# A hybrid trunk layer: input products made of un-normalised h, with the norm's factor applied where each block leaves PSUM

## The chip, the core and the metric

The kernel runs on one core of one Trainium2 chip. A core has TensorE (PE in the profile; PEld is its weight load), VectorE (DVE), ScalarE (ACT), GpSimd (POOL) and SyncE (SP, which here only issues the transfers), each with its own instruction queue that runs in order. The metric is the device time of one execution in microseconds.

## The reference, cut to what matters

One layer over T = 528 tokens (16 learned ones and 512 of the sequence), 1024 channels wide:

```python
u = rmsnorm(h, norm_mix[l])               # h * rsqrt(mean(h*h) + eps) * gain
proj = u @ w_in[l]
feat_rw, feat_fx, gate_part = ...         # recurrent group, attention group, gates
gates = sigmoid(gate_part + b_gate[l])
y_rw = rwkv7_branch(feat_rw, ...)         # begins f + mu * (token_shift(f) - f)
y_fx = fox_branch(feat_fx, ...)           # q and k get a head rmsnorm
merged = gates[..., :D] * (y_rw @ w_out_rw[l]) + gates[..., D:] * (y_fx @ w_out_fx[l])
h = h + merged @ w_o[l]
h = h + square(relu(rmsnorm(h, norm_mlp[l]) @ w_up[l])) @ w_down[l]
```

The factor of rmsnorm is one number per token. A product with u is therefore the product with gain * h, times that number for each token. Channels lie on partitions and tokens along the columns, so the factor is a row of T numbers, the same on all partitions.

## The kernel before, in words

**Precision.** Every large product takes both operands as a high and a low part (`whi`, `wlo`, `uhi`, `ulo`) and three passes: high by high, high by low, low by high. The high part is a copy on ACT, the low part a subtraction on DVE or GpSimd.

**Blocks.** The input projection is cut into 42 blocks of 128 output channels: two lora blocks (`B_LORA`, `B_GD`), then for each of four pairs of heads three attention blocks (query, key, value) and three recurrent ones (key, receptance, value: tiles `okk`, `orr`, `ov`), then 16 gate blocks. A block is 8 k-slices x 3 passes per part of the tokens. A part is 264 columns (HT), so two parts make a block; gates and queries take one part of 512. PSUM has two banks for them (`ppj`, tag "pj").

**Opening (L304 to L402).** For each half of the tokens: squares on ACT (L332), sums of them on DVE (L339, L342), h times the gain split into `uhi` and `ulo` (L335, L336), the forget products `pf` (L347), the sum over channels by a product with ones (L350), and the factor `rs` as Ln and Exp on ACT (L352, L353). The first two blocks are made of this un-normalised h and multiplied by `rs` in PSUM (L361). Then h is normalised in place, and split once more (L371 to L374), for all other blocks. The first two blocks pass Tanh (L399, L400), are split into `lhi` and `llo`, and feed the lora products of `decay` (L680).

```python
V.scalar_tensor_tensor(xt[t][:, k, :], xt[t][:, k, :], pr[:, ...], rss[t], ALU.mult, ALU.mult)   # L371
A.copy(uhi[:, kk, tk], xt[t][:, kk, :])                                                          # L373
V.tensor_tensor(ulo[:, kk, tk], xt[t][:, kk, :], uhi[:, kk, tk].bitcast(F32), ALU.subtract)      # L374
```

**Token shift (L297 to L300).** A recurrent block leaves PSUM in two steps: ACT writes mu * block into a tile `tm`, one column to the right (L298), and DVE adds (1 - mu) * block to it (L299).

**Middle.** Several streams of work run beside one another: `recurrent` (decay, keys, rows, scores, the inverse of a triangular matrix, bonus), `chain` (the recurrence over nine chunks), `group_norm`, `fox_features`, `attention`, and `projections`, which makes the asked blocks by rank: recurrent first, attention next, gates last (L446 to L475). `Turns` writes PE's order from them: a model clock (`Clock`) guesses when each step's inputs are ready, and the stream of the best rank that can go on is written next. The order on PE is then fixed (`manual_schedule`), while the other engines' instructions are placed by the scheduler, with more priority for streams of rank 0 and 1. Gates are stored to DRAM with their bias added (L481, L482).

**Merge (L1021 to L1038).** For each of 8 blocks m and both branches (br), a gate is loaded (`gl`, two buffers for each branch), passes Tanh, and is multiplied with the branch's product `po` (four PSUM buffers); GpSimd adds the branches and the sum is split.

```python
nc.sync.dma_start(g, gates_d[8 * br + m])                                   # L1026
act(g, g, AF.Tanh, scale=0.5)                                               # L1027
...                                                                         # 12 products into po, L1032
V.scalar_tensor_tensor(g, g, 1.0, po, ALU.add, ALU.mult)                    # L1034
...
G.tensor_tensor(pp[0], pp[0], pp[1], ALU.add)                               # L1036
merged = act(mhi[:, m, :], pp[0], AF.Copy, scale=0.5)                       # L1037
V.scalar_tensor_tensor(mlo[:, m, :], pp[0], 0.5, mhi[...], ALU.mult, ALU.subtract)   # L1038
```

The product with w_o (L1064) follows, whose four results take the four `po` buffers, then its second half (L1081) and the MLP (L1115, L1148).

Of the kernel before, what the change touches and what calls it, by code (L numbers as in the profile page):

```python
# [182 lines left out]
def kernel(ctx, tc, ht, x, win, par, cst, gain, lora, wout, wo, wup, wdn, out, dbg=None):  # L183
# [20 lines left out]
    pr1 = cp.tile([128, 14], F32, name="pr1")  # L204
    prh = cp.tile([128, 4, 4], F32, name="prh")
# [57 lines left out]
    with ExitStack() as st:  # L263
# [13 lines left out]
        def proj(blk, evac, parts=((0, HT), (HT, T)), w=None):  # L277

            w = w or load_w(win[blk], (G, V))
            for a0, a1 in parts:  # L280
                po = ppj("pj")[:, :a1 - a0]
                n = 0
                for k in range(KB):
                    for a, b in passes(wk(w, k), U):
                        mm(po, a, b[:, k, a0:a1], start=n == 0, stop=n == 23)
                        n += 1
                evac(po, slice(a0, a1))

# [3 lines left out]
        def tshift(blk, dst):  # L292

            tm = rp.tile([128, 1 + T], F32, name="tm")
            V.memset(tm[:, 0:1], 0.0)

            def evac(po, sl):  # L297
                act(tm[:, sl.start + 1:sl.stop + 1], po, AF.Copy, scale=pr[:, C_MU + blk:C_MU + blk + 1])  # L298
                V.scalar_tensor_tensor(dst[:, sl], po, pr1[:, blk:blk + 1], tm[:, sl], ALU.mult, ALU.add)  # L299
            return evac  # L300

# [10 lines left out]
        lfs = [rp.tile([128, TP], F32, name=f"lf{i}", tag=("okk", "orr")[i]) for i in range(2)]  # L312
        with tc.tile_pool(name="xp", bufs=2) as xp:
# [3 lines left out]
            nc.sync.dma_start(pr, par)  # L317
            for c in range(4):
                nc.sync.dma_start(xt[0][:, 2 * c:2 * c + 2, :].rearrange("p a b -> p (a b)"), ht[0, c])
            w_lora = load_w(win[B_LORA], (G, G))  # L320
            for c in range(4):
                nc.sync.dma_start(xt[1][:, 2 * c:2 * c + 2, :].rearrange("p a b -> p (a b)"), ht[1, c])
            w_gd = load_w(win[B_GD], (G, G))
# [3 lines left out]
            rss = []  # L327
            for t in range(2):
                tk = slice(HT * t, HT * t + HT)
                for c in range(4):  # L330
                    sq = xp.tile([128, 2, HT], F32, name="sq", bufs=3)
                    act(sq, xt[t][:, 2 * c:2 * c + 2, :], AF.Square)  # L332
                    for k in range(2 * c, 2 * c + 2):
                        gn = pr[:, C_GN + k:C_GN + k + 1]
                        act(uhi[:, k, tk], xt[t][:, k, :], AF.Copy, scale=gn)  # L335
                        V.scalar_tensor_tensor(ulo[:, k, tk], xt[t][:, k, :], gn, uhi[:, k, tk].bitcast(F32), ALU.mult, ALU.subtract)  # L336
                    if c == 0:
                        acc = xp.tile([128, HT], F32, name="acc")
                        V.tensor_tensor(acc, sq[:, 0, :], sq[:, 1, :], ALU.add)  # L339
                    else:  # L340
                        for k in range(2):
                            V.tensor_tensor(acc, acc, sq[:, k, :], ALU.add)  # L342
                pf = psm("pf")[:8, :HT]
                n = 0
                for k in range(KB):
                    for a, b in passes([x[:, 8 * k:8 * k + 8] for x in wf], U):
                        mm(pf, a, b[:, k, tk], start=n == 0, stop=n == 23)  # L347
                        n += 1
                pq = psm("pss")[:, :HT]
                mm(pq, ones, acc, start=True, stop=True)  # L350
                rs = xp.tile([128, HT], F32, name="rs")
                act(rs, pq, AF.Ln, bias=eps, scale=1.0 / 1024)  # L352
                act(rs, rs, AF.Exp, scale=-0.5)  # L353
                rss.append(rs)
                V.tensor_tensor(f0[:, tk], pf, rs[:8], ALU.mult)
                if t == 0:
                    V.tensor_scalar(pr1, pr[:, C_MU:C_MU + 14], -1.0, 1.0, ALU.mult, ALU.add)
                    shift = tshift(12 + B_LORA, lfs[0])

                def normed_shift(po, sl):  # L360
                    V.tensor_tensor(po, po, rss[sl.start // HT], ALU.mult)  # L361
                    shift(po, sl)

                proj(B_LORA, normed_shift, ((tk.start, tk.stop),), w_lora)
            shift = tshift(12 + B_GD, lfs[1])
            proj(B_GD, normed_shift, w=w_gd)
            for t in range(2):
                tk = slice(HT * t, HT * t + HT)
                for c in range(4):
                    for k in range(2 * c, 2 * c + 2):  # L370
                        V.scalar_tensor_tensor(xt[t][:, k, :], xt[t][:, k, :], pr[:, C_GN + k:C_GN + k + 1], rss[t], ALU.mult, ALU.mult)  # L371
                    kk = slice(2 * c, 2 * c + 2)
# [858 lines left out]
```

## Time and profile before

| | |
|---|---|
| median of 3 runs | 937.02 us (935.64 to 938.87) |
| the profiled execution's own time | 937.56 us |
| its span in the trace | 935.6 us |
| mean granted PE clock | 0.967 |
| PE busy | 882.0 us, 94% |
| first block product of the middle | at 42.76 us |
| first product of the merge | at 486.76 us |
| first product of the MLP (L1115) | at 581.24 us |

Times are microseconds from the start of the span. A row of a timeline gives start, length, engine, line and operation, then output and inputs by the program's names, and in brackets how long the engine idled before and what it waited for. A row of groups gives the count after x, the busy time, and the mean in ns. Matmuls are pipelined: the distance from one start to the next counts, not a row's length. "Clock" is the share of full speed that PE was granted.

### The profile page before, as it was taken

Reading aid. Unit: us, or ns where it says so; the run is one execution under the profiler, and the core shown is the slowest. Engines: PE = TensorE matmul, PEld = TensorE weight load, DVE = VectorE, ACT = ScalarE, POOL = GpSimd, SP = SyncE. Lnnn points to the kernel's source line nnn. Section 1 sums busy time; section 2 is a strip of 40 time slices with the busy share of each in tenths; the row PEclk is TensorE's granted clock in tenths of the full one; section 3 lists DMA queues with packets and bytes.
Section 4 is the critical chain, followed back from the end, with each engine's and each line's share of the span. In section 5 each row is a group of like instructions: output and inputs, shape, how many; then the busy total and the mean of one; then the engine's idle time right before and its main releaser. Section 6 shows DMA issues by size and latency. Waiting matters only on the chain.

```text
span 935.6 us, 15452 instructions
## 1 busy us (share of the span) xinstructions
PE 882.0 (94%) x5964; PEld 721.1 (77%) x5964; DVE 515.2 (55%) x1052; ACT 422.3 (45%) x885; POOL 158.3 (17%) x145
## 2 busy tenths in 40 slices
PE   6589889999888999999979999999999999999998
PEld 4578777688777778678758778988888888888886
DVE  7974875548869861663356755354423244443322
ACT  7746342677354535746454553344322233442221
POOL 4253333213232332113302200000000000000000
PEclk9789899899889999999989999999999999999999
DMA  5121112111011132112247650122232222222331
GB/s 204 46 69 47 46 49 86 58 58 45 28 46 35 61 117 81 47 58 90 80 154 262 212 174 9 43 94 101 90 102 93 99 101 92 101 98 94 119 118 57
DMA packets 45449, 83.30 MB, mean 89 GB/s; under 512 B 5048, under 2 KB 6200, under 8 KB 45376
## 3 DMA queue, kind: packets, MB, share of 16 engines
q1 hardware_dynamic: 45376, 82.32, 25.8%
q8 instruction: 47, 0.77, 0.3%
q14 instruction: 26, 0.21, 0.1%
HBM read 75.99 MB, written 6.31 MB: 88 GB/s over the span
## 4 chain that ended last, share of the span: by engine, by line
PE 79%; DVE 12%; ACT 3%; DMA 3%; issue 2%; POOLq 0%; SPq 0%; DVEq 0%; ACTq 0%
PE pj L470 21%; PE po L1115 19%; PE pd L1148 19%; PE po L1032 4%; PE po L1081 2%; PE pw L822 2%; PE psc L574 1%; PE py L619 1%; DVE xt L371 1%; DVE L L726 1%; DVE L L724 1%; PE ppt L605 1%; PE pbt L770 1%; PE pch L887 1%; PE psr L755 1%
## 5 line engine op out<-in xcount | busy, mean ns | idle before, releaser
L231 DVE TENSOR_TENSOR wlo<-wraw,whi 128x512 fp32r<-128x512 f32 x148 | 104.9, 710 | 177.1 <-ACT whi L230 175.2
L230 ACT CAST whi<-wraw 128x512 fp32r<-128x512 f32 x152 | 94.0, 620 | 192.1 <-PE pd L1148 109.6
L470 PE MATMUL pj<-uhi,whi 128*128 128x264 f32 (+1 forms) x480 | 169.5, 353 | 3.8 <-DVE orr L299 2.6
L470 PE MATMUL pj<-uhi,wlo 128*128 128x264 f32 (+1 forms) x480 | 158.7, 331 | 0.0
L470 PE MATMUL pj<-ulo,whi 128*128 128x264 f32 (+1 forms) x480 | 158.6, 330 | 0.0
L442 POOL TENSOR_TENSOR wlo<-wraw,whi 128x512 fp32r<-128x512 f32 x80 | 108.4, 1359 | 251.6 <-ACT whi L441 244.1
L470 PEld LDWEIGHTS pj<-uhi,whi 128*128 128x128 f32 x480 | 94.8, 197 | 24.1 <-issue 10.6
L470 PEld LDWEIGHTS pj<-uhi,wlo 128*128 128x128 f32 x480 | 94.6, 197 | 7.2
L1148 PE MATMUL pd<-whi,fhi 128*128 128x512 f32 x256 | 99.6, 389 | 0.0
L1148 PE MATMUL pd<-wlo,fhi 128*128 128x512 f32 x256 | 99.6, 389 | 0.0
L1148 PE MATMUL pd<-whi,flo 128*128 128x512 f32 x256 | 99.6, 389 | 0.0
L470 PEld LDWEIGHTS pj<-ulo,whi 128*128 128x128 f32 x480 | 95.2, 198 | 4.9
L1115 PE MATMUL po<-zhi,whi 128*128 128x512 f32 (+1 forms) x248 | 94.8, 382 | 0.0
L1115 PE MATMUL po<-zlo,whi 128*128 128x512 f32 (+1 forms) x248 | 94.8, 382 | 0.0
L1115 PE MATMUL po<-zhi,wlo 128*128 128x512 f32 (+1 forms) x248 | 94.8, 382 | 0.0
L441 ACT CAST whi<-wraw 128x512 fp32r<-128x512 f32 x80 | 49.5, 619 | 57.1 <-PE pj L470 36.4
L1148 PEld LDWEIGHTS pd<-wlo,fhi 128*128 128x128 f32 x256 | 48.1, 188 | 10.0
L1148 PEld LDWEIGHTS pd<-whi,fhi 128*128 128x128 f32 x256 | 48.1, 188 | 10.0
L1148 PEld LDWEIGHTS pd<-whi,flo 128*128 128x128 f32 x256 | 48.1, 188 | 9.9
L1115 PEld LDWEIGHTS po<-zlo,whi 128*128 128x128 f32 x248 | 46.6, 188 | 9.1
L1115 PEld LDWEIGHTS po<-zhi,whi 128*128 128x128 f32 x248 | 46.6, 188 | 9.0
L1115 PEld LDWEIGHTS po<-zhi,wlo 128*128 128x128 f32 x248 | 46.6, 188 | 9.0
(277 smaller groups left out, 1461.6 us busy)
## 6 DMA issues: line engine op xcount, KB each, us to landing
wraw<-in_win SPq DMA_DIRECT2D x84, 256.0 KB, 2.6
wraw<-in_wup SPq DMA_DIRECT2D x64, 256.0 KB, 2.6
wraw<-in_wdn SPq DMA_DIRECT2D x64, 256.0 KB, 2.5
gd<-gt SPq DMA_DIRECT2D x16, 256.0 KB, 2.1
wraw<-in_wout SPq DMA_DIRECT2D x16, 256.0 KB, 4.0
gl<-gd SPq DMA_DIRECT2D x16, 256.0 KB, 3.4
wraw<-in_wo SPq DMA_DIRECT2D x16, 256.0 KB, 3.3
xt<-in_ht SPq DMA_DIRECT2D x8, 264.0 KB, 4.6
```

Source lines behind the costliest of these rows:

```text
L230: A.copy(hi, raw)
L231: low.tensor_tensor(lo, raw, hi.bitcast(F32), ALU.subtract)
L371: V.scalar_tensor_tensor(xt[t][:, k, :], xt[t][:, k, :], pr[:, C_GN + k:C_GN + k + 1], rss[t], ALU.mult, ALU.mult)
L441: A.copy(hi, raw)
L442: G.tensor_tensor(lo, raw, hi.bitcast(F32), ALU.subtract)
L470: mm(po, a, b[:, k, a0:a1], start=n == 0, stop=n == 23)
L574: mm(sc, q[hs, 128 * i:128 * i + 128], k[hs, a:b], start=True, stop=True)
L822: mm(ps_[hs, n - b0, :], lhs(n)[hs], rhs(n)[hs], start=True, stop=True)
L1032: mm(po, a, b[:, k, :], start=n == 0, stop=n == 11)
L1081: mm(po, a[:, k, 128 * i:128 * i + 128], b[:, k, :], start=n == 0, stop=n == 23)
L1115: mm(po[:, t0:t1], a, b[:, k, t0:t1], start=n == 0, stop=n == 23)
L1148: mm(pd[i], a[:, b_, 128 * i:128 * i + 128], b, start=b_ == 0 and n == 0, stop=b_ == 15 and n == 2)
```

## The change

The in-place normalisation goes, and `uhi`, `ulo` stay un-normalised for all blocks. The factor `rs` is kept for all T tokens and applied

- to recurrent blocks by DVE in PSUM, ahead of the token shift; the shift now has ACT write (1 - mu) * block and DVE add mu times the column to the left, in place, without `tm`. So the second part starts two columns earlier (`SHIFTED`);
- to query, key and value blocks by DVE on the way out of PSUM (queries and keys are squared from SBUF after it);
- to gates after they are loaded back, by GpSimd; their bias moves into Tanh's bias operand (`bgh`).

In the opening the two lora blocks and the forget products are made together, k-slice by k-slice, in an order written out by hand (PE's manual order now begins there), the second half of tokens in the two banks that the recurrence uses later; weights are loaded in between h's slices, and DVE makes their low parts. Every block's evacuation gets the scheduler's priority, the model clock is read around it, the lora products wait in the model for `lhi` and `llo` (set to 5.0), and the inverse gives way to other streams at every second step.

```diff
+    bgh = cp.tile([128, 16], F32, name="bgh")
+    rs = cp.tile([128, T], F32, name="rs")
...
             def evac(po, sl):
-                act(tm[:, sl.start + 1:sl.stop + 1], po, AF.Copy, scale=pr[:, C_MU + blk:C_MU + blk + 1])
-                V.scalar_tensor_tensor(dst[:, sl], po, pr1[:, blk:blk + 1], tm[:, sl], ALU.mult, ALU.add)
+                n, x = sl.stop - sl.start, 2 if sl.start else 0
+                V.tensor_tensor(po, po, rs[:, sl], ALU.mult)
+                act(dst[:, sl.start + x:sl.stop], po[:, x:], AF.Copy, scale=pr1[:, blk:blk + 1])
+                x = x or 1
+                d = dst[:, sl.start + x:sl.stop]
+                V.scalar_tensor_tensor(d, po[:, x - 1:n - 1], pr[:, C_MU + blk:C_MU + blk + 1], d, ALU.mult, ALU.add)
             return evac
+        manual = st.enter_context(ExitStack())
+        manual.enter_context(tc.manual_schedule(engines={mybir.EngineType.PE}))
...
+            load_x(0, 0)
+            w2 = [[], []]
+            for j in range(2):
+                for i, blk in enumerate((B_LORA, B_GD)):
+                    w2[i].append(load_h(win[blk][:, 512 * j:512 * j + 512], V, "w", (4, 4, 4)))
+                load_x(0, 1 + j)
+            load_x(0, 3)
             for c in range(4):
+                load_x(1, c)
...
+                    for j in range(3):
+                        for a, b, dst, cols in [(*passes([x[:, 8 * k:8 * k + 8] for x in wf], U)[j], pf, tk)] + [(*passes(wk(w2[i], k), U)[j], pls[i], sl) for i in range(2)]:
+                            mm(dst, a, b[:, k, cols], start=n == 0, stop=n == 23)
                         n += 1
...
+                for j in range(2):
+                    mm(pq, ones, acc[:, j, :], start=j == 0, stop=j == 1)
+                act(rs[:, tk], pq, AF.Ln, bias=eps, scale=1.0 / 1024)
+                act(rs[:, tk], rs[:, tk], AF.Exp, scale=-0.5)
...
-            for t in range(2):
-                tk = slice(HT * t, HT * t + HT)
-                for c in range(4):
-                    for k in range(2 * c, 2 * c + 2):
-                        V.scalar_tensor_tensor(xt[t][:, k, :], xt[t][:, k, :], pr[:, C_GN + k:C_GN + k + 1], rss[t], ALU.mult, ALU.mult)
-                    kk = slice(2 * c, 2 * c + 2)
-                    A.copy(uhi[:, kk, tk], xt[t][:, kk, :])
-                    V.tensor_tensor(ulo[:, kk, tk], xt[t][:, kk, :], uhi[:, kk, tk].bitcast(F32), ALU.subtract)
...
+        for t_ in (lhi, llo):
+            ck.w[t_.tensor.name] = 5.0
...
+        SHIFTED = ((0, HT), (HT - 2, T))
...
-                        evac(po, slice(a0, a1))
+                        ck.read()
+                        ck.urgent = True
+                        with tc.high_priority():
+                            evac(po, slice(a0, a1))
+                        ck.read()
+                        ck.urgent = False
...
-                    act(gt, po, AF.Identity, bias=pr[:, C_BG + i:C_BG + i + 1])
+                    A.copy(gt, po)
...
-                            d["s"] = act(sq[:, sl], po, AF.Square)
-                            A.copy(f[:, sl.start - c0:sl.stop - c0], po)
+                            x = f[:, sl.start - c0:sl.stop - c0]
+                            V.tensor_tensor(x, po, rs[:, sl], ALU.mult)
+                            d["s"] = act(sq[:, sl], x, AF.Square)
...
-                    return lambda po, sl: A.copy(d["v"][:, sl], po)
+                    return lambda po, sl: V.tensor_tensor(d["v"][:, sl], po, rs[:, sl], ALU.mult)
...
-                    yield lambda: max(ck.ready(*lw), banks(2))
+                    yield lambda: max(ck.ready(*lw, lhi, llo), banks(2))
...
             for s in range(15):
+                if s % 2:
+                    yield lambda: ck.ready(AX_) - 2.0
...
                 nc.sync.dma_start(g, gates_d[8 * br + m])
-                act(g, g, AF.Tanh, scale=0.5)
+                G.tensor_tensor(g, g, rs[:, NM:], ALU.mult)
+                act(g, g, AF.Tanh, bias=bgh[:, 8 * br + m:8 * br + m + 1], scale=0.5)
```

More of the change, by code (lines that the diff above doesn't have):

```diff
@@ L275 @@
         U = (uhi, ulo)
[L277 to L286, printed above, removed]
-                evac(po, slice(a0, a1))
         SEQ = ((NM, T),)
@@ L311 @@
         f1 = rp.tile([8, T], F32, name="f1", tag="sq")
-        lfs = [rp.tile([128, TP], F32, name=f"lf{i}", tag=("okk", "orr")[i]) for i in range(2)]
+        lfs = [rp.tile([128, T], F32, name=f"lf{i}", tag=("okk", "orr")[i]) for i in range(2)]
         with tc.tile_pool(name="xp", bufs=2) as xp:
@@ L326 @@
             split(wf[0], wf[1], pr[:, C_FL:])
-            rss = []
+            V.tensor_scalar(pr1, pr[:, C_MU:C_MU + 14], -1.0, 1.0, ALU.mult, ALU.add)
+            shifts = [tshift(12 + blk, lfs[i]) for i, blk in enumerate((B_LORA, B_GD))]
             for t in range(2):
                 tk = slice(HT * t, HT * t + HT)
-                for c in range(4):
-                    sq = xp.tile([128, 2, HT], F32, name="sq", bufs=3)
-                    act(sq, xt[t][:, 2 * c:2 * c + 2, :], AF.Square)
-                    for k in range(2 * c, 2 * c + 2):
[L334 to L342, printed above, removed]
+                sl = slice(tk.start - 2 * t, tk.stop)
@@ L348 @@
                         n += 1
                 pq = psm("pss")[:, :HT]
[L350 to L358, printed above, removed]
@@ L375 @@
+                act(rs[:, tk], pq, AF.Ln, bias=eps, scale=1.0 / 1024)
+                act(rs[:, tk], rs[:, tk], AF.Exp, scale=-0.5)
+                V.tensor_tensor(f0[:, tk], pf, rs[:8, tk], ALU.mult)
+                for i in range(2):
+                    shifts[i](pls[i], sl)
         y_rw = yp.tile([128, 4, S], F32, name="y_rw")
@@ L381 @@
         V.tensor_scalar(prh[:, 3, :], pr[:, C_KA:C_KA + 4], -0.5, 1.0, ALU.mult, ALU.add)
+        V.tensor_scalar(bgh, pr[:, C_BG:C_BG + 16], 0.5, None, ALU.mult)
         V.tensor_scalar(qg8, pr[:, C_QG:C_QG + 1], 0.125, None, ALU.mult)
@@ L395 @@
         dump("F", fF)
-        lf, gf = (x[:, :T] for x in lfs)
+        lf, gf = lfs
         act(lf[:64], lf[:64], AF.Tanh)
@@ L658, in begin @@
                     return tshift(3 * self.p + i, pad(t))
-                return ask(1, self.b0 + i, begin, need=need)
+                return ask(1, self.b0 + i, begin, SHIFTED, need)
             def ask_keys(self, need=None):
@@ L995 @@
             ask(9, B_GATE + i, gate_job(i), SEQ)
-        with tc.manual_schedule(engines={mybir.EngineType.PE}):
-            turns.run()
+        turns.run()
+        manual.close()
         dump("y_rw", y_rw.rearrange("p a b -> p (a b)"))
```

31 lines of the change are left out of this document (14 added, 17 removed).

## The prediction

> **What bounds the kernel now.** I read the engine table first, then the chain that ended last, then the stretches between the stage borders, then what TensorE (PE) waits for.
>
> ```profile
> PE 882.0 (94%) x5964; PEld 721.1 (77%) x5964; DVE 515.2 (55%) x1052; ACT 422.3 (45%) x885; POOL 158.3 (17%) x145
> PE 79%; DVE 12%; ACT 3%; DMA 3%; issue 2%; POOLq 0%; SPq 0%; DVEq 0%; ACTq 0%
> ```
>
> PE is busy for 94% of the span and holds 79% of the chain, so time can be won or lost only where PE idles or runs at a low clock. The stretches say where. Columns: length, then busy time (and instructions) of PE, weight load, VectorE (DVE), ScalarE (ACT), GpSimd (POOL), then granted clock.
>
> ```profile
> 0.00:42.70 42.70, 23.43 (x160) 17.93 (x160) 36.89 (x83) 31.34 (x60) 14.43 (x21) 0.93 0.40 137
> 42.70:482.20 439.50, 414.88 (x3782) 334.97 (x3780) 277.01 (x670) 225.14 (x537) 132.13 (x116) 0.94 0.18 59
> 482.20:600.00 117.80, 112.01 (x562) 93.78 (x563) 69.52 (x105) 58.48 (x112) 11.75 (x8) 0.97 0.46 158
> 600.00:935.60 335.60, 331.70 (x1464) 274.40 (x1462) 131.75 (x196) 107.29 (x179) 0.00 (x0) 1.00 0.29 98
> ```
>
> PE idles 42.7 - 23.4 = 19.3 us in the opening, 24.6 us in the long middle, 5.8 us around the merge, and little after 600, where nothing of the change lies. The change can touch three stretches: it shortens the opening, puts multiplications into the middle, and puts a GpSimd multiplication into the merge.
>
> **The opening, -2.9 us.** Removed are the lines that normalise h in place.
>
> ```profile
> L371 DVE SCALAR_TENSOR_TENSOR xt<-xt,pr,rs 128x264 f32<-128x264 f32 x16 | 10.0, 660 | 0.0
> L374 DVE TENSOR_TENSOR ulo<-xt,uhi 128x528 fp32r<-128x528 f32 x8 | 5.5, 694 | 0.0
> ...
> L361 DVE TENSOR_TENSOR pj<-pj,rs 128x264 f32<-128x264 f32 x4 | 1.7, 428 | 0.0
> ```
>
> ```profile
> 41.37 0.59 PE L680 MATMUL pup<-llo,lw 64*128 64x264 f32 x2 [7.72 <-DVE llo L255]
> 42.76 0.59 PE L470 MATMUL pj<-uhi,whi 128*128 128x264 f32 x1
> ```
>
> That is 15.5 us of DVE work, in front of llo, for which PE waits 7.72 us; the first block product starts at 42.76. It is not 15.5 us of time, because other things are late next. First, PE: the changed opening has the same 144 products, now strictly in one order, each block's k-slices for all three targets, and four sums of squares instead of two.
>
> ```profile
> 5.77 0.39 PE L347 MATMUL pf<-uhi,wf 128*8 128x264 f32 x1 [5.77 <-ACT uhi L335]
> ...
> 25.02 0.28 PE L285 MATMUL pj<-uhi,whi 128*128 128x264 f32 x1
> ...
> 27.44 0.28 PE L285 MATMUL pj<-uhi,wlo 128*128 128x264 f32 x1
> ```
>
> ```profile
> L335 ACT ACTIVATE uhi<-xt,pr 128x264 fp32r<-128x264 f32 x16 | 7.3, 504 | 0.0
> ...
> L332 ACT ACTIVATE sq<-xt 128x528 f32<-128x528 f32 x8 | 5.1, 635 | 1.3 <-DMA xt<-in_ht 1.3
> ```
>
> From 25.02 to 27.44 are 20 steps, 0.121 us each. 144 such are 17.4 us; from the same start at 5.8, with about 2 us for the four sums and 2.5 us for the slow first products and the first weights' split (an estimate), PE ends near 27.7. ACT's 12.4 us of squares and splits and four weight casts are done near 19, so they, DVE's splits (four weight splits come over to it from GpSimd), and h's slices, which SP now loads behind the weights, all hide under PE. Then comes a serial ACT chain, in the compiled order: Ln, Exp, (DVE multiplies), the bias, two shifts, Exp, table load, Tanh, table load, Ln, table load, Tanh, the split.
>
> ```profile
> 25.10 0.48 ACT L352 ACTIVATE rs<-pss,eps 128x264 f32<-128x264 f32 x1 [0.25 <-PE pss L350]
> ...
> 29.31 1.28 ACT L399 ACT_TABLE_LOAD   x1
> 30.61 0.65 ACT L399 ACTIVATE lf<-lf 64x528 f32<-64x528 f32 x1
> ```
>
> Three loads of 1.28, some eight activations of 0.45 to 0.65 and three DVE steps of 0.4 to 0.7 make about 10.7: llo near 38.4. The twelve lora products ahead of the first block product took 42.76 - 41.37 = 1.4, so it starts at 39.85, 2.9 us sooner. The weights of the first blocks are converted by then on ACT and GpSimd. Bounds: -6 if PE warms at once and the chain overlaps, -0.5 if the cold start lasts. PE still waits some 10 us there, so the slow restart stays:
>
> ```profile
> 43.15 0.42 PE L470 MATMUL pj<-ulo,whi 128*128 128x264 f32 x1
> ...
> 46.89 0.41 PE L470 MATMUL pj<-uhi,whi 128*128 128x264 f32 x1
> ```
>
> Seventeen steps of 0.22 instead of 0.121: 1.7 us, spent now and after. The Trainium skill (TensorE: Matmul & The Clock Gate, "HAM oscillation") says that idle gaps of over about 3.4 us throttle PE, and the trace agrees: a wait of 7.72 us, then half speed. By that rule a long wait that the change adds costs some 2 us more than itself; that lies inside my bounds below.
>
> **The middle, -1.2 us.** Every block leaving PSUM is now multiplied by the factor on DVE: 24 recurrent parts and 16 key and value parts at 0.43 (L361), 4 query blocks of twice the width (by the same rate 0.8): 20 us more DVE on top of 277.0 of 439.5, while ACT loses its plain copies. A part takes 24 x 0.121 = 2.9 us on PE, there are two banks, and the evacuation (DVE, ACT, DVE instead of ACT, DVE) still fits when DVE is free; behind a long DVE instruction it doesn't. Where DVE is already the limit PE waits:
>
> ```profile
> PE psr L755 <- DVE L L726: 1.5, 1, 1.5
> PE pj L470 <- DVE orr L299: 1.3, 1, 1.3
> PE psr L755 <- DVE L L759: 0.8, 1, 0.8
> ```
>
> The compiled PE order answers partly: 138 block products instead of 126 stand ahead of the first pair's score products, 120 instead of 114 ahead of the second's: 18 x 0.121 = 2.2 us of filled wait. The value copy, for which PE waited 3.0 (below), moves to DVE with priority: I take half, 1.5. Against it I set 2.5 us for DVE's 20: it runs 63% busy over the stretch, and an eighth of the added work is what I let meet a waiting PE, the 0.26 us that two more columns in 288 products cost among it. The evacuations wait for PE at the head of DVE's queue, with the inverse's and the rows' instructions behind them. Bounds: -8 (a third of the 24.6 us idle goes), +8 (four tenths of the added work is late).
>
> ```profile
> PE pv L544 <- ACT vf L533: 3.0, 1, 3.0
> ```
>
> **Into the merge, +1.5 us.** PE's order now ends the middle with 45 gate products after the last attention product; before, the last attention followed the last gate.
>
> ```profile
> 480.88 0.69 ACT L481 ACTIVATE gt<-pj,pr 128x512 f32<-128x512 f32 x1 [0.96 <-PE pj L470]
> ...
> 486.09 0.62 ACT L230 CAST whi<-wraw 128x512 fp32r<-128x512 f32 x1 [0.22 <-DMA wraw<-in_wout]
> ```
>
> ```profile
> 486.76 0.80 PE L1032 MATMUL po<-yhi,whi 128*128 128x512 f32 x1 [4.59 <-ACT whi L230]
> ```
>
> The merge's first weights are loaded on SP's queue behind the last gate's store, in both kernels. From the last gate's evacuation to the first merge product took 486.76 - 480.88 = 5.9 us, of which PE waited 4.59 and had 1.3 of attention. Now it has none of that, and waits it all. Bounds 0 to +2.
>
> **The merge, +7.5 us.** The factor is applied to each gate by GpSimd. Two multiplications per m are 16 more of the size of its addition, and the compiled GpSimd order puts the addition of m behind the multiplication of m+1 (m from 1 to 4). That multiplication waits for a DMA into the buffer that m-1 gives back only after its addition, mhi and mlo: a ring, once per m.
>
> ```profile
> L1027 ACT ACTIVATE gl<-gl x16: 615/632/636, 488.9 to 531.7; 128x512 f32<-128x512 f32 x16
> ...
> L1036 POOL TENSOR_TENSOR gl<-gl,gl x8: 1276/1446/1799, 495.3 to 535.5; 128x512 f32<-128x512 f32 x8
> L1037 ACT ACTIVATE mhi<-gl x8: 615/628/635, 497.0 to 537.2; 128x512 fp32r<-128x512 f32 x8
> L1038 DVE SCALAR_TENSOR_TENSOR mlo<-gl,mhi x8: 684/692/693, 497.6 to 537.8; 128x512 fp32r<-128x512 f32 x8
> ...
> DMA to landing us min/median/max: 2.5/3.4/5.7
> ```
>
> ```profile
> 495.34 1.60 POOL L1036 TENSOR_TENSOR gl<-gl,gl 128x512 f32<-128x512 f32 x1 [31.18 <-DVE gl L1034]
> 500.71 1.29 POOL L1036 TENSOR_TENSOR gl<-gl,gl 128x512 f32<-128x512 f32 x1 [3.77 <-DVE gl L1034]
> ```
>
> By the medians (the middle ones of three, in ns) a turn is 0.63 + 0.69 + 3.4 + 1.45 + 1.45 and 0.1 of hops, 7.7 us. PE needs less per m:
>
> ```profile
> 532.39 0.39 PE L1064 MATMUL po<-whi,mhi 128*128 128x512 f32 x1
> ...
> 534.25 0.50 PE L1064 MATMUL po<-whi,mhi 128*128 128x512 f32 x1 [0.34 <-DVE gl L1034]
> ```
>
> 192 products from 486.76 to 532.39, 45.6 us, about 5.5 per m once warm (24 steps of 0.228). The first addition ends 10.2 us into the stage (495.34 + 1.60 - 486.76). Four turns of 7.7 give 41.0; the loads, multiplications and additions of m 5 to 7 follow at 47.4 and 53.7, the last multiplication at 55.2, Tanh and the two last products with po at 57.9. Four po buffers hide this from PE until m is 6 or so, but L1064 needs all four at its start (the 0.34 above is already that wait). Its last 87 products take 19.8 us: end at 77.7, against 68.0 now: +9.7. With a landing of 3.0 (towards the shortest) and GpSimd at its shortest, 1.28, the same sum gives +5.2; I take 7.5, between them, as DMA is less busy there without the loads of x, which come earlier now. At the shortest of all rows (2.5 and 1.28) it is +2.2, at GpSimd's longest (1.8) +14.
>
> ```profile
> L231 DVE TENSOR_TENSOR wlo<-wraw,whi 128x512 fp32r<-128x512 f32 x148 | 104.9, 710 | 177.1 <-ACT whi L230 175.2
> ```
>
> ```profile
> 500.76 1.79 DVE L231 TENSOR_TENSOR wlo<-wraw,whi 128x512 fp32r<-128x512 f32 x1
> ```
>
> The weight split beside a GpSimd addition took 1.79 us against a mean of 0.71: it waited for GpSimd, so the new multiplications also delay weights, and may be held up themselves (rival 5). The Trainium skill (SBUF — State Buffer, "Who interferes with whom") calls this an exclusive lock between GpSimd and a DVE instruction with two SBUF inputs, whole instructions long. This row agrees; by that rule, held throughout, the stage would take the long GpSimd durations, +14 instead of +7.5.
>
> **Sum.** -2.9 - 1.2 + 1.5 + 7.5 = +4.9 us on the profiled execution's own 937.56 (span 935.6 and 2.0 around it): 942.5. That execution lies 0.5 above the median of 937.02, so for the median I say 942.0.
>
> **Rivals.**
> 1. The middle pays: PE's new order and evacuations with priority remove waits and slow restarts that I left standing. For it: 24.6 us of idle, and clocks below 0.95 beside each wait. Against it: DVE, the engine waited for, gets 20 us more. It decides from about -8 in the middle with a ring at its short rows: -2.9 - 8 + 1.5 + 2.2 = -7.2, 930, faster.
> 2. The terms cancel: the ring costs 5.2 or less and the middle gives 3: -2.9 - 3 + 1.5 + 5 = +0.6, 938.
> 3. DVE becomes the bound of the middle: its heavy parts are full (9.39 of 10 us at 100 to 110), and +8 there gives 951 with the ring.
>
> ```profile
> 100.00:110.00 10.00, 6.85 (x57) 6.03 (x57) 9.39 (x14) 2.06 (x4) 4.56 (x6) 0.93 0.17 53
> ```
>
> 4. The opening gains nothing, since PE's cold start or the table loads take it all: 945, with the ring.
> 5. GpSimd and DVE hold each other up through the merge, each GpSimd instruction at its longest, 1.8: +14 there, 948.5.
>
> **Numbers.** A measurement of this kernel can tell about 0.3% (2.8 us) from no change. Forecast 942, with the ring as worked out: 0.38; rival 1: 0.27; rival 2: 0.20; rivals 3 and 4: 0.08 together; rival 5: 0.07. The forecast's lower edge reaches into no change, so: faster 0.27, the same 0.23, slower 0.50. Leaving out about a tenth on each side, rival 1's far part and that of rivals 3 and 5, the range is 929 to 951.
>
> **What would show it.** Opening: the first block product near 39.9 (right), under 37 or over 42 (wrong). Middle: its idle near 24 us, the wait for the value copy halved. Merge: GpSimd's additions 7 to 8 us apart, PE waiting for DVE's gl at the start of L1064 (L1066 in the new file) for several us; if that wait is under 2 us, the ring is wrong, and the kernel is level or faster. A first merge product less than 5 us after the last gate product would refute the third term.

## The result, and the profile after

The changed kernel takes **964.17 us** (962.75 to 965.86) against 937.46 for the kernel before on the same chips: ratio 1.028, 95% interval 1.025 to 1.031. It is 26.7 us slower. The forecast was 942.0 (929 to 951): the sign is right, the size is not.

The engine table and the chain of the changed kernel, to be held against those of before (882.0 us of PE, 94%; DVE 12% of the chain):

```profile
PE 888.8 (92%) x5968; PEld 724.1 (75%) x5968; DVE 525.4 (55%) x1055; ACT 413.3 (43%) x857; POOL 172.4 (18%) x157
...
PE 76%; DVE 14%; ACT 3%; DMA 2%; issue 2%; POOL 2%; SPq 0%; DVEq 0%; ACTq 0%; POOLq 0%
```

The span grew by 28.3 us and PE's busy time by 6.8, so most of the loss is waiting. I cut the span at three events: the first block product, the first merge product, and the first product of the second half of w_o. Between the first two lies the **middle**, between the last two the **merge**. Columns as in the prediction: length, busy time of PE, weight load, DVE, ACT, GpSimd, granted clock. Middle and merge of the kernel before:

```profile
42.80:486.80 444.00, 414.82 (x3783) 334.97 (x3781) 281.62 (x677) 229.33 (x545) 132.13 (x116) 0.94 0.18 62
486.80:556.00 69.20, 68.11 (x289) 55.07 (x289) 43.96 (x64) 37.65 (x64) 11.75 (x8) 0.97 0.66 227
```

Opening, middle, merge and rest of the changed kernel:

```profile
0.00:40.30 40.30, 23.44 (x164) 19.87 (x164) 23.27 (x56) 29.38 (x55) 8.12 (x18) 0.88 0.44 145
40.30:504.10 463.80, 417.66 (x3783) 335.08 (x3781) 302.38 (x707) 224.25 (x528) 135.64 (x119) 0.94 0.19 63
504.10:584.40 80.30, 72.27 (x288) 56.24 (x289) 47.99 (x64) 36.80 (x61) 28.64 (x20) 0.93 0.56 180
584.40:963.90 379.50, 375.46 (x1737) 312.92 (x1736) 151.79 (x229) 122.84 (x216) 0.00 (x0) 1.00 0.27 89
```

The opening gives 2.4 us, the middle costs 19.8 and the merge 11.1; the rest is level. In the middle DVE has 20.8 us more, as the prediction counted, and PE idles 46.1 us instead of 29.2. The four largest of PE's waits there (total, times, longest):

```profile
PE psr L754 <- DVE BK L713: 7.2, 2, 3.6
PE pv L543 <- DVE vf L532: 5.6, 2, 3.1
PE psr L754 <- DVE L L758: 5.5, 6, 1.2
PE ppt L602 <- DVE rsum L588: 4.9, 1, 4.9
```

All of these name DVE. In the kernel before, PE waited 3.0 us for the value copy (`vf`), and not at all for the keys (`BK`). The next rows show the fourth wait. PE, in the changed kernel, around the first inverse, and the edges of opening and merge:

```profile
37.79 0.59 PE L679 MATMUL pup<-lhi,lw 64*128 64x264 f32 x2 [10.03 <-ACT lhi L256]
...
40.33 0.59 PE L462 MATMUL pj<-uhi,whi 128*128 128x264 f32 x1
...
144.57 0.55 PE L543 MATMUL pv<-cs,vf 128*128 128x128 f32 x3 [3.09 <-DVE vf L532]
155.60 0.37 PE L602 MATMUL ppt<-cs,pe 128*16 128x128 f32 x1 [4.87 <-DVE rsum L588]
...
504.08 0.79 PE L1034 MATMUL po<-yhi,whi 128*128 128x512 f32 x1 [6.17 <-ACT whi L232]
```

DVE at the same place:

```profile
146.34 4.49 DVE L817 COPY Tt<-TT 32x576 f32<-32x576 f32 x4
150.84 2.60 DVE L817 COPY AX<-AX 32x576 f32<-32x576 f32 x4
...
153.68 0.49 DVE L582 TENSOR_TENSOR psc<-psc,cs 128x128 f32<-128x128 f32 x2
...
154.96 0.16 DVE L588 RECIPROCAL rsum<-rsum 128x1 f32<-128x1 f32 x1 [0.35 <-ACT pe L587]
```

The inverse gave way, so PE's order has the first attention step of pair 0 inside it; but on DVE that attention's scores stand behind the inverse's last copies, and PE stands still until 155.60, in front of a product that nothing can pass.

### The profile page after: what moved, and what is told of

The parts are those of the page before. It is cut to its first block, busy times and chain, and to the rows that moved or that the text cites. A ratio compares the mean times of both kernels' runs of the same rounds, so it can differ in the third digit from the quotient of the medians.

```text
span 963.9 us, 15442 instructions
## 1 busy us (share of the span) xinstructions
PE 888.8 (92%) x5968; PEld 724.1 (75%) x5968; DVE 525.4 (55%) x1055; ACT 413.3 (43%) x857; POOL 172.4 (18%) x157
## 4 chain that ended last, share of the span: by engine, by line
PE 76%; DVE 14%; ACT 3%; DMA 2%; issue 2%; POOL 2%; SPq 0%; DVEq 0%; ACTq 0%; POOLq 0%
PE pj L462 19%; PE po L1117 18%; PE pd L1150 18%; PE po L1066 2%; PE po L1083 2%; DMA gl<-gd 2%; PE pw L823 1%; DVE tmp L805 1%; DVE AX L806 1%; PE psc L573 1%; DVE L L723 1%; POOL gl L1028 1%; PE py L618 1%; POOL gl L1038 1%; DVE Bm L757 1%
## 5 line engine op out<-in xcount | busy, mean ns | idle before, releaser
L233 DVE TENSOR_TENSOR wlo<-wraw,whi 128x512 fp32r<-128x512 f32 x152 | 108.6, 715 | 182.4 <-ACT whi L232 180.8
L462 PE MATMUL pj<-uhi,whi 128*128 128x264 f32 (+2 forms) x480 | 170.4, 355 | 2.4 <-DVE orr L291 2.4
L462 PE MATMUL pj<-ulo,whi 128*128 128x264 f32 (+2 forms) x480 | 158.6, 330 | 0.0
L462 PE MATMUL pj<-uhi,wlo 128*128 128x264 f32 (+2 forms) x480 | 158.1, 329 | 0.0
L462 PEld LDWEIGHTS pj<-uhi,whi 128*128 128x128 f32 x480 | 94.3, 197 | 22.0 <-issue 10.2
```

The costliest lines, as they stand in the source:

```text
L233: low.tensor_tensor(lo, raw, hi.bitcast(F32), ALU.subtract)
```

## The experiments

Times are medians; ratios are to the kernel before on the same chip (937.5 to 938.9 us), with 95% intervals. Stages come from one profiled execution each, which in e3 and e18 was some 5 us shorter than the median, and in e10 and e16 8 and 4 us longer: they show the place, the median the price. Opening, middle and merge are as above.

| run | us | ratio (interval) | opening | middle | merge |
|---|---|---|---|---|---|
| before | 937.5 | | 42.8 | 444.0 | 69.2 |
| changed | 964.2 | 1.028 (1.025-1.031) | 40.3 | 463.8 | 80.3 |
| e1 | 965.2 | 1.029 (1.024-1.034) | 40.5 | 461.1 | 80.4 |
| e2 | 954.3 | 1.018 (1.015-1.021) | 40.6 | 453.7 | 77.9 |
| e3 | 973.6 | 1.037 (1.033-1.042) | 41.1 | 465.1 | 80.6 |
| e4 | 955.4 | 1.018 (1.013-1.022) | 41.9 | 461.7 | 69.8 |
| e5 | 952.6 | 1.016 (1.013-1.019) | 40.8 | 461.1 | 68.9 |
| e6 | 948.1 | 1.010 (1.007-1.013) | 40.9 | 458.2 | 68.3 |
| e7 | 954.4 | 1.017 (1.015-1.020) | 43.1 | 459.6 | 70.6 |
| e8 | 945.6 | 1.008 (1.006-1.010) | 40.5 | 454.9 | 68.8 |
| e9 | 938.6 | 1.001 (0.999-1.002) | 42.7 | 446.3 | 70.3 |
| e10 | 973.3 | 1.039 (1.035-1.044) | 42.8 | 487.1 | 69.8 |
| e11 | 944.8 | 1.008 (1.007-1.010) | 43.0 | 441.5 | 79.4 |
| e12 | 946.8 | 1.011 (1.009-1.013) | 41.4 | 456.0 | 67.8 |
| e13 | 945.6 | 1.008 (1.006-1.010) | 42.8 | 454.7 | 69.4 |
| e14 | 942.7 | 1.005 (1.003-1.006) | 42.7 | 449.9 | 69.0 |
| e15 | 944.8 | 1.007 (1.005-1.008) | 41.3 | 452.2 | 68.9 |
| e16 | 986.9 | 1.050 (1.048-1.052) | 41.0 | 487.6 | 80.7 |
| e17 | 948.8 | 1.012 (1.009-1.015) | 40.4 | 448.4 | 77.7 |
| e18 | 949.9 | 1.012 (1.010-1.015) | 41.7 | 444.1 | 77.3 |

### First: load, order, priority, merge

Theory A was that DVE's added work itself costs the middle; theory B that the new order does.

**e1**, a thin factor (8 of a recurrent part's columns are multiplied, the others left as they are):

```diff
-                V.tensor_tensor(po, po, rs[:, sl], ALU.mult)
+                c = n if blk >= 12 else 8
+                V.tensor_tensor(po[:, :c], po[:, :c], rs[:, sl.start:sl.start + c], ALU.mult)
```

> Recurrent blocks are multiplied by the factor in 8 of their 264 columns only (the rest of the factor is left out for them), while the planner's model is still charged for the whole width, so that PE's order stays that of the changed kernel, instruction for instruction; about 8 us of DVE's work in the middle go. Theory A (the middle's 17 us come from DVE's added work, met by a waiting PE): the middle of 456.8 us gets 5 to 10 us shorter, 954 to 959 in all. Theory B (they come from PE's new order, above all the inverse that gives way and the evacuations with priority; the work itself is hidden): at most 2 us, 962 to 964.

DVE lost 7.9 us in the middle (302.38 to 294.47), the middle 2.7, the median nothing. Theory A falls as far as the recurrent blocks' load goes.

**e2**, no giving way:

```diff
             for s in range(15):
-                if s % 2:
-                    yield lambda: ck.ready(AX_) - 2.0
```

> The inverse no longer gives way at every second step, as in the kernel before; all else as changed. Theory A: the middle stays within 3 us of 456.8, 961 to 967 in all. Theory B: 8 us or more come back, under 956.

The middle lost 10.1 us, and the wait of 4.87 is gone. The median, 954.3, is as theory B had it.

**e3**, no priority (the bare `evac(po, slice(a0, a1))` again):

> Evacuations without the scheduler's priority and without the reading of the model clock around them, as in the kernel before. Theory A: no gain, or a loss, since the longer evacuation then waits behind other DVE work: 962 to 970. Theory B: DVE's rows, keys and inverse are no longer pushed back, the middle gets 6 us or more shorter, under 958.

9 us slower by the median, 2 by its profiled execution, so the priority is no cost here. Theory B is right on the giving way alone.

**e4**, gates early:

```diff
                     A.copy(gt, po)
+                    G.tensor_tensor(gt, gt, rs[:, NM:], ALU.mult)
...
-                G.tensor_tensor(g, g, rs[:, NM:], ALU.mult)
                 act(g, g, AF.Tanh, bias=bgh[...], scale=0.5)
```

> GpSimd multiplies each gate by the factor before it is stored, in the middle, instead of after it is loaded back in the merge; PE's order is the same, instruction for instruction. If the ring on GpSimd is what makes the merge longer (80.3 us from its first product to the first of the w_o product's second half, 69.2 before), the stage comes back to 69 to 71 and the whole gains 9 to 11 less what 21 us of added GpSimd work cost the middle: 953 to 957. If the merge is longer because its weights come late or the clock is low, the stage stays above 76 and the whole above 960.

The merge is back at 69.8. The ring is all but 0.6 us of the merge's loss. GpSimd in the merge of the changed kernel, two turns of it:

```profile
532.19 1.29 POOL L1028 TENSOR_TENSOR gl<-gl,rs 128x512 f32<-128x512 f32 x1 [2.83 <-DMA gl<-gd]
534.12 1.30 POOL L1028 TENSOR_TENSOR gl<-gl,rs 128x512 f32<-128x512 f32 x1 [0.64 <-DMA gl<-gd]
535.38 1.74 POOL L1038 TENSOR_TENSOR gl<-gl,gl 128x512 f32<-128x512 f32 x1
539.94 1.29 POOL L1028 TENSOR_TENSOR gl<-gl,rs 128x512 f32<-128x512 f32 x1 [2.83 <-DMA gl<-gd]
541.93 1.28 POOL L1028 TENSOR_TENSOR gl<-gl,rs 128x512 f32<-128x512 f32 x1 [0.69 <-DMA gl<-gd]
543.17 1.73 POOL L1038 TENSOR_TENSOR gl<-gl,gl 128x512 f32<-128x512 f32 x1
```

Addition to addition takes 7.79 us. GpSimd idles 2.83 in each turn for a load that could only be issued after the last addition.

### Second: do the pieces add up?

**e5**, e2 and e4 together. **e6**, e5 without the factor. **e8**, e5 with queries and keys unscaled (evacuation as before: Square and copy on ACT).

> The two edits that helped, together: the inverse doesn't give way, and gates are multiplied by the factor before they are stored. If they are separate costs, the gains of 9.8 and 8.8 us add up: 944 to 947. If the GpSimd work that comes into the middle collides with the inverse or the weight splits there, less than 14 of the 18.6 are seen: over 950.

> As the kernel with both edits, but the factor is left out for all recurrent, query, key and value blocks; queries, keys and values leave PSUM on ACT as in the kernel before; evacuations keep their priority. Theory A (what is left of the middle's loss, 8 to 10 us, is the multiplications in the evacuation): the middle up to the merge takes at most 446 us, 935 to 939 in all. Theory D (it is the rest of the new order and the priority): it stays above 450, 942 to 947.

> As the kernel with both edits, but queries and keys leave PSUM without the factor (Square and copy on ACT, as in the kernel before): their own head norm divides it out again, up to its eps. 6.6 us of DVE's work go. Theory A: a third of the remaining loss comes back, 941 to 944. Theory D: no change against the kernel with both edits, 944 to 947.

They don't add up: e5 has the merge of e4 but a middle of 461.1, 7.4 more than e2, though GpSimd's 21 us cost nothing beside the giving way (e4). Leaving out all multiplications (18 us of DVE) brings only 2.9 back (e6; 4.5 by the medians), nearer to theory D; leaving out those of queries and keys alone brings 6.2 (e8; 7.0 by the medians). A piece's price depends on the order that it meets. So I turned round and put single parts into the kernel before.

**e7**, the giving way alone in the kernel before (the two lines of e2):

> The kernel before, with one edit of the change alone: the inverse gives way at every second step. If the giving way is a cost of its own, the middle up to the merge (444.0 us) gets 7 to 12 us longer, 945 to 950 in all. If it costs only beside longer evacuations, it stays within 3 us: 935 to 941.

15.6 us in the middle, a cost of its own, and more than either forecast. Here it falls elsewhere. PE, then the granted clock in the stretches behind it:

```profile
223.02 0.28 PE L470 MATMUL pj<-uhi,wlo 128*128 128x264 f32 x1
230.53 1.06 PE L942 MATMUL pyt<-cs,y_rw 128*64 128x128 f32 x4 [7.23 <-DVE y_rw L935]
```

```profile
217.00:223.00 6.00, 6.00 (x70) 5.18 (x69) 4.57 (x11) 5.11 (x15) 1.46 (x2) 1.00 0.01 3
...
233.00:235.50 2.50, 1.71 (x18) 1.14 (x18) 1.19 (x4) 0.53 (x2) 0.00 (x0) 0.50 0.00 0
235.50:238.00 2.50, 2.50 (x27) 1.97 (x24) 0.58 (x2) 1.07 (x5) 0.00 (x0) 0.50 0.00 0
```

PE's order now has the group norm's transposes early, while DVE is still on keys and the norm's small steps; 7.23 us of waiting, then half clock.

### Third: one part alone in the kernel before

**e9**, the new opening alone, with h normalised in place behind it:

> The kernel before with the new opening alone: lora blocks and forget products made together in the written order, weights between h's slices; h is then normalised in place as before, and PE's order of the middle is that of the kernel before, instruction for instruction. If the opening's gain of 2.4 us is its own, the first block product starts at 40 to 41 and the whole takes 934 to 936.5. If the in-place normalisation, left standing, holds llo or the first slices up, it starts after 42.3 and the whole takes 937 or more.

The gain is gone: first block product at 42.7. The rows of PE say why: `lhi` comes 1.1 us later than in the changed kernel (38.92, not 37.79), and the wait for `llo` behind it is 1.77, not 0.55, because ACT and DVE also normalise.

```profile
38.92 0.59 PE L683 MATMUL pup<-lhi,lw 64*128 64x264 f32 x2 [10.12 <-ACT lhi L254]
41.28 0.59 PE L683 MATMUL pup<-llo,lw 64*128 64x264 f32 x2 [1.77 <-DVE llo L255]
42.68 0.59 PE L473 MATMUL pj<-uhi,whi 128*128 128x264 f32 x1
```

**e10**, the multiplications alone (by one):

```diff
+                if blk < 12:
+                    V.tensor_tensor(po, po, one..., ALU.mult)
                 act(tm[:, sl.start + 1:sl.stop + 1], po, AF.Copy, scale=...)
...
-                            d["s"] = act(sq[:, sl], po, AF.Square)
-                            A.copy(f[...], po)
+                            V.tensor_tensor(x, po, one..., ALU.mult)
+                            d["s"] = act(sq[:, sl], x, AF.Square)
...
-                    return lambda po, sl: A.copy(d["v"][:, sl], po)
+                    return lambda po, sl: V.tensor_tensor(d["v"][:, sl], po, one..., ALU.mult)
```

> The kernel before with the multiplications alone: every recurrent, query, key and value block is multiplied by one on DVE where it leaves PSUM (in PSUM ahead of the token shift; on the way to SBUF for the others, in place of ACT's copy), 20 us more of DVE's work, nothing else changed. Theory A (the work on DVE costs by itself): the middle up to the merge, 444.0 us, gets 4 to 9 us longer, 941 to 947. If the cost lies in the giving way alone: at most 2 us, 936 to 940.

Neither theory: 43 us in the middle for 14 us more of DVE (36 us by the medians). What PE waited for, and the place:

```profile
PE pw L827 <- DVE AX L821: 29.0, 4, 15.7
```

```profile
130.00:140.00 10.00, 3.37 (x28) 3.15 (x26) 9.13 (x28) 4.04 (x6) 2.65 (x2) 0.82 0.16 52
140.00:150.00 10.00, 0.44 (x2) 0.29 (x2) 9.67 (x17) 0.59 (x2) 1.41 (x1) 0.50 0.05 13
```

For over 15 us PE has nothing to do but wait for the inverse (`pw` is its first product). In the compiled order of the kernel before, 138 block products (135 for the second inverse) stand between the last bonus product and that place; here it is 30 and 66. The planner's reason, read from its code and not tested by itself: there are two PSUM banks for blocks, the attention blocks now leave them by DVE, and DVE is booked with the inverse, so no further block could begin. This is **theory P**: the multiplications cost not by their length but by the banks that they keep while DVE is on the inverse, and priority or giving way are two remedies for that, each with a price.

**e11**, one GpSimd multiplication per gate in the merge:

> The kernel before with one multiplication (by one) on GpSimd for each gate after it is loaded back, PE's order unchanged. If the ring is the whole cost of the merge: first merge product to the second half of the w_o product 79 to 81 us instead of 69.2, 947 to 949 in all. If part of the 11 us came from the changed kernel's other state (weights late, clock): under 75, under 944.

Merge 79.4: the ring alone is 10.2 us. The whole grew by 7.3 only, since the middle of this execution was 2.5 shorter.

**e12**, e8 with the gates multiplied by DVE on the way out of PSUM:

> From the changed kernel: the inverse doesn't give way, queries and keys leave PSUM without the factor (their head norm divides it out up to its eps), and DVE multiplies each gate by the factor as it leaves PSUM, in place of ACT's copy, with nothing on GpSimd. If the GpSimd multiplications were what cost the middle 7 us in the run with both edits, this one takes 936 to 941. If 16 gate evacuations of 0.7 to 0.8 on DVE cost as much, 943 or more.

No better than e8 (middle 456.0). The gates' place is not what keeps these middles above 450.

### Fourth: theory P

**e13**, **e14**: priority in the kernel before, alone and with the multiplications of e10. **e15**: the changed kernel without giving way and without any factor. **e16**: the changed kernel with neither remedy.

> The kernel before with the evacuations' priority alone (and the reading of the model clock around them). Theory P (priority is a remedy that costs little by itself): the middle up to the merge stays within 4 us of 444.0, 935 to 941. Theory Q (pushing evacuations ahead of keys, rows and inverse on DVE is what costs the last 8 to 10 us): it takes 450 or more, 944 and up.

> The kernel before with the multiplications by one and the evacuations' priority. In PE's order 141 and 138 block products stand again between the last bonus product and the inverse's first product, where the multiplications alone left 30 and 66. Theory P: the waits of 29 us for the inverse go, the middle takes 450 to 456, 943 to 949. If the multiplications cost by DVE's load whatever the order: over 960.

> The changed kernel with its opening, shift and priority, but the inverse doesn't give way and the factor is left out for every block, gates too. Theory P: the last 8 to 10 us of the middle's loss are the multiplications, so the middle takes 442 to 448 and the whole 932 to 938. Theory Q: it stays above 451, over 941.

> The changed kernel with neither the giving way nor the priority; all multiplications stay. In PE's order only 30 and 42 block products stand between the last bonus product and the inverse's first product (141 and 138 with priority alone), because blocks can't leave PSUM while DVE is on the inverse. If that is what the multiplications cost: PE waits 25 to 40 us at the inverse's first products, 975 to 995. If not: within 5 us of the 973.6 that the kernel without priority took or faster than it.

e16 shows the banks' wait in the changed kernel:

```profile
PE pw L816 <- DVE AX L810: 31.5, 4, 15.7
```

Priority takes it away: e14 has all multiplications, 37 us less than e10 in the middle (31 by the medians), and is only 4 us (1.005) slower than the kernel before. But priority has a price of its own, 10.7 us of middle in e13 (7 by the medians), so theory P's "costs little" is wrong, and theory Q right there. e15 points the same way: with no factor at all the middle is still 452.2, though it holds the change's opening, shift and priority together.

**e17**: no remedy, but the attention blocks leave PSUM on ACT (values as below, queries and keys without the factor), and gates have four load buffers. **e18**: the same with two buffers, and DVE multiplying the gates in the merge.

```diff
-                    return lambda po, sl: V.tensor_tensor(d["v"][:, sl], po, rs[:, sl], ALU.mult)
+                    return lambda po, sl: A.copy(d["v"][:, sl], po)
...
-                A.copy(vt.rearrange("p a b -> p (a b)"), pv)
+                for j in range(4):
+                    act(vt[:, j, :], pv[:, 128 * j:128 * j + 128], AF.Copy, scale=rT[:, j:j + 1])
```

> The changed kernel with neither the giving way nor the priority, but the attention blocks leave PSUM on ACT alone, as in the kernel before: queries and keys without the factor (their head norm divides it out up to its eps), values with it after their transpose, where tokens lie on partitions and ACT takes it as a scale per partition (five small transposes of the factor in the opening). Recurrent blocks keep their multiplication on DVE; gates have four load buffers per branch. PE's order has 141 and 147 block products ahead of the inverse's first product, with no remedy. If the multiplications cost by keeping PSUM's banks while DVE is on the inverse: no wait over 2 us at the inverse's first products, the middle up to the merge 444 to 450; with the ring loosened by the buffers the merge takes 69 to 73: 934 to 943. If any multiplication on DVE without priority starves PE: middle over 456, over 946.

> The same, but with two load buffers for the gates and DVE in place of GpSimd multiplying them in the merge (16 times 0.7 us, DVE busy 44 of 69 us there). The middle as in the run beside it. If the ring needs GpSimd's 1.3 us turns: merge 69 to 72, 934 to 942 in all. If the wait for the loaded buffer now stands ahead of DVE's weight splits: merge over 75, over 943.

Middle and merge of e18:

```profile
41.70:485.80 444.10, 411.57 (x3783) 332.80 (x3781) 289.57 (x691) 233.71 (x560) 132.93 (x115) 0.95 0.21 66
485.80:563.10 77.30, 71.41 (x289) 57.22 (x290) 50.20 (x76) 36.63 (x61) 11.95 (x8) 0.92 0.60 188
```

The middle is 448.4 in e17, within its forecast, and 444.1 in e18, with no priority and no giving way, where e16 has 487.6. The 444.1 is partly luck: this execution of e18 was the fastest of six, and by the medians both kernels lose some 4 us outside opening and merge. PE's waits for the inverse are 0.2 us in e18 and none in e17, and 141 and 147 block products stand ahead of its first products in e17, where e16 has 30 and 42. That shows that it was the attention blocks on DVE, and e14, with all the work on DVE and no such waits, that it wasn't the load; that they act through the two banks is the planner's reason, as theory P has it. The merge stays at 77: four buffers don't loosen the ring (e17), and it doesn't need GpSimd (e18). In e17's compiled order the additions simply moved back with the buffers: eight multiplications, then the first addition, and each addition behind the multiplications of three blocks later, whose loads wait for the addition before. GpSimd in e17, 7.71 us from addition to addition:

```profile
513.68 1.74 POOL L1040 TENSOR_TENSOR gl<-gl,gl 128x512 f32<-128x512 f32 x1
518.23 1.29 POOL L1030 TENSOR_TENSOR gl<-gl,rs 128x512 f32<-128x512 f32 x1 [2.81 <-DMA gl<-gd]
520.14 1.29 POOL L1030 TENSOR_TENSOR gl<-gl,rs 128x512 f32<-128x512 f32 x1 [0.62 <-DMA gl<-gd]
521.39 1.74 POOL L1040 TENSOR_TENSOR gl<-gl,gl 128x512 f32<-128x512 f32 x1
```

No version beats the kernel before; e9 equals it. The opening of e17, the middle of e18 and the merge of e12 (40.4, 444.1, 67.8) with a rest of 379.5 would make a span of 931.8, but that kernel was not run, e18's middle is that of its fastest execution, and e5 shows that such sums can fail. Open is also why orders with priority end at middles of 450 to 461 whatever else they hold.

## Why the prediction was wrong

**The opening, -2.9: right.** The first block product came at 40.33 (forecast 39.85). PE ended at 27.76 (37.79 less 10.03; forecast 27.7) and waited for ACT's chain. The first product with `llo` came at 38.93 (forecast 38.4), and from there to the first block product it took the 1.4 us of the forecast.

**The middle, -1.2: the step that failed.** With the wait ahead of the merge kept apart it became +18.2. What failed is what I booked as gains of the new order, and what I gave no price.

- "18 x 0.121 = 2.2 us of filled wait": the 18 products do stand there, but the first waits of the two pairs' score products went from 1.50 each to 3.59 and 3.57 (the 7.2 us for `BK` above), because DVE has the keys ready later. With no factor they are 0.8 (e15), without priority no wait for the keys is left there (e3), and with the thin factor they are 4.3 (e1): it takes multiplications and priority together, and it isn't their length. Why the two together delay the keys is open.
- "I take half, 1.5", for the value copy: the wait grew from 3.0 to 5.6.
- The inverse's giving way had no price. It costs 10.1 in the changed kernel (e2) and 15.6 alone (e7), since it moves PE's products ahead of what DVE, in its own order, can feed.

The other 8 or so fit the priority by e13 (10.7 alone) and e15 (8.2), but e14, with priority and multiplications, has 5.9, so how they divide is open.

"An eighth of the added work is what I let meet a waiting PE", +2.5, prices DVE's 20 us by length. In size this came near what the changed kernel shows (2.7 of middle for 7.9 us in e1, though nothing by its median; 2.9 for 18 in e6 against e5). But it holds only beside remedies that the sum gave no price: without them the multiplications cost 43 us of middle (e10), where the step bounded it by +8, from a share of the added work, and no share of 20 us gives 43. What counts is which work stands ahead of an evacuation on its engine.

Rival 3 (DVE becomes the bound) had the right engine and sign, and neither the mechanism nor the size: DVE is busy for 302 of 464 us.

**Into the merge, +1.5: right.** The wait grew from 4.59 to 6.17.

**The merge, +7.5: right mechanism, too small.** It was +11.1. Four turns take 7.2 to 7.8 us each, as worked out from the medians (7.7), whose sum gave +9.7; I took less on the guess that loads would land sooner and GpSimd run at its shortest. Loads do land in 2.9 us and the multiplications take 1.30, but an addition's median rose from 1.45 to 1.67, and the turn stayed. The waits at the first products of w_o:

```profile
PE po L1066 <- DVE gl L1036: 2.9, 1, 2.9
PE po L1066 <- ACT whi L232: 1.5, 1, 1.5
PE po L1066 <- DVE wlo L233: 1.2, 1, 1.2
```

The sum by medians had PE go on with the last `gl` 57.9 us into the stage, and it did so at 57.6 (561.71). What that sum lacked comes behind it: it counted the products there at full speed, but ten steps took 4.4 us instead of 2.3, at half clock. PE, then the granted clock:

```profile
561.71 0.80 PE L1066 MATMUL po<-whi,mhi 128*128 128x512 f32 x1 [2.88 <-DVE gl L1036]
562.31 0.63 PE L1066 MATMUL po<-wlo,mhi 128*128 128x512 f32 x1
...
566.15 0.49 PE L1066 MATMUL po<-wlo,mhi 128*128 128x512 f32 x1
```

```profile
560.00:570.00 10.00, 8.29 (x27) 6.57 (x28) 5.29 (x8) 4.90 (x7) 1.84 (x2) 0.68 0.33 107
```

All of this comes with the ring: without it the merge is 69.8 (e4).

Rival 5 (every GpSimd instruction at 1.8, +14) comes near in time, but only in part by its mechanism: the additions ran at 1.67, the multiplications at 1.30.

The two buffers, named as part of the ring, aren't its cause (e17).

## What to carry to other kernels

When an evacuation moves to another engine, ask first which long in-order stretch it will stand behind there and how many PSUM banks are left meanwhile; its own duration says little (by the medians, 6 to 8 us of DVE for the recurrent blocks go with a loss of some 4 us in e17 and e18, and 14 us with the attention blocks cost 36 in e10). Where PE's order is fixed ahead, each remedy that changes it has its own price, so measure every remedy alone, in the kernel before too. A multiplication between a load and the use of its buffer made a ring here, on GpSimd and on DVE; more buffers moved it (e17), and putting the multiplication ahead of the store removed it (e4).

## What the runs showed of the hardware

The inverse's small DVE steps of 0.27 us took 1.25 beside a GpSimd weight split. DVE and then GpSimd in the changed kernel:

```profile
131.33 0.27 DVE L805 TENSOR_TENSOR tmp<-AX 128x110 f32<-128x110 f32 x1
131.64 1.25 DVE L806 TENSOR_TENSOR AX<-AX,tmp 128x110 f32<-128x110 f32 x1
```

```profile
131.41 2.73 POOL L434 TENSOR_TENSOR wlo<-wraw,whi 128x512 fp32r<-128x512 f32 x2 [6.22 <-ACT whi L433]
```

The second step began inside the split and took about a microsecond longer; the step behind it took 1.36. This agrees with the exclusive lock of the Trainium skill (SBUF — State Buffer, "Who interferes with whom"): here each of two short steps of a serial chain paid most of a GpSimd instruction.

A wait of 3.09 us ahead of 144.57 left the granted clock at 1.00, and one of 4.87 ahead of 155.60 halved it:

```profile
144.50:147.00 2.50, 2.43 (x14) 1.85 (x15) 2.49 (x3) 1.08 (x4) 0.47 (x1) 1.00 0.00 0
...
155.50:158.00 2.50, 2.40 (x7) 2.04 (x8) 1.40 (x4) 1.27 (x4) 1.28 (x1) 0.50 0.51 188
```

The bound of about 3.4 us of the Trainium skill (TensorE: Matmul & The Clock Gate, "HAM oscillation") lies between the two. The length of one wait isn't all, though: in the merge a wait of 2.88, with waits of 1.54 and 1.18 in the 6 us before it, was enough for the half clock shown above.
